# Six matmuls of two k-tiles in another order, in a hybrid decoder step

## The chip, the cores and the metric

The kernel runs on one core of one Trainium2 chip. The metric is the time of one execution in device microseconds, taken over several runs; beside it there is one execution that was recorded by the hardware profiler, with the instructions of every engine.

## The reference

The kernel computes one layer of a hybrid decoder for a prompt of 256 tokens and for 8 samples of 4 tokens, 288 token rows together, with a model width of 2048. Nearly all of its arithmetic is products of the token rows with float32 weights:

```python
xn = _rmsnorm(x, p['norm_mix'])
z, xbc, dt_raw, q, k, v, r, g_lr, gate_a, gate_b = _split(xn @ p['w_in'], IN_SIZES)
...
branch_a = u @ p['w_ssd_out']
...
branch_b = o @ p['w_gla_out']
merged = jax.nn.sigmoid(gate_a) * branch_a + jax.nn.sigmoid(gate_b) * branch_b
h = x + merged @ p['w_mix_out']
h = h + _cross_attend(_rmsnorm(h, p['norm_cross']), mem_k, mem_v, p['w_cq'], p['w_co'])
up = _rmsnorm(h, p['norm_ffn']) @ p['w_up']
...
h = h + (jax.nn.silu(gt) * a) @ p['w_down']
```

Between them stand two recurrences (a state-space scan and gated linear attention), cross-attention into 256 memory tokens, whose keys and values are projections of 256 memory rows, and a causal convolution in the feed-forward part.

## The kernel before, in words

**Three products for one.** TensorE multiplies in the reduced format float32r. To keep float32 accuracy, each operand is split into a high part (the value rounded to float32r) and a low part (the rest, rounded too), and a product becomes three: high by high, high by low, low by high, added up in one PSUM accumulator. The token rows are split once for a stage: `X(k)` gives the pair `xh`, `xl` of k-tile `k`, each 128 x 288. The weights are split as they come: `wload` (L102) brings a block of up to four k-tiles by 256 columns into one of three `raw` buffers by SyncE's queue, and `wsplit` (L94) makes two k-tiles of it into `hi`, a copy on ScalarE (L97), and `lo`, a subtraction on VectorE (L99). There are five buffers for each.

**The loop.** `proj_w` (L114) is a generator for one projection of at most 256 output columns, that is `nt` = 2 accumulators of 128 output columns by 288 token rows, each in a PSUM bank. For each pair of k-tiles it splits the weights and then, for each accumulator, issues six matmuls (L127 to L133). The weights are the stationary operand, 128 x 128, the token rows are streamed, 288 of them. A group of six is called a group in what follows; two groups use one split, and twelve matmuls thus use one `hi` and one `lo`. After the last pair of k-tiles `cons` takes the accumulator out. `yield` after each split lets `weave` (L154) put pieces of the scans or of attention between the groups.

**The order of the work.** Everything on an engine runs in the order of the program; waits between engines are set by a framework, from the tiles that an instruction reads and writes. A `hi` buffer comes free after the last matmul that reads it, and ScalarE then makes the next split into it. Four accumulators rotate, so that one projection can start while the one before is taken out.

**Where it is used.** All projections of token rows run through `proj_w`: `w_in` (rows `xn`), the two output projections of the branches (`un`, 4 k-tiles at a time), `w_mix_out` (`mx`), `w_cq` (`hn`), `w_co` (`co`), `w_up` (`hf`) and `w_down` (`pr`). The projections of the memory rows have a loop of their own, `mem_proj` (L287), in which the rows are the stationary operand and 512 columns of the weights are streamed; the change doesn't touch it. Cross-attention multiplies split operands as well, 256 columns at a time (L1346 to L1348, L1387 to L1389).

In the profile a matmul's operands are named with the streamed one first: `acc<-hf,whi` streams `hf` through the stationary `whi`.

Of the kernel before, what the change touches and what calls it, by code (L numbers as in the profile page):

```python
# [40 lines left out]
def hybrid_step(ctx: ExitStack, tc: tile.TileContext, I: dict, O: list):  # L41
# [3 lines left out]
    MM, TR = nc.tensor.matmul, nc.tensor.transpose  # L45
# [10 lines left out]
    def acc_tile():  # L56
        return ps.tile([P, 512], F32, tag="acc", bufs=4, name="acc")

    def mm_tile():
        return ps.tile([P, 512], F32, tag="mm", bufs=3, name="mm")  # L60
# [33 lines left out]
    def wsplit(raw):  # L94

        hi = wp.tile(list(raw.shape), F32R, tag="whi", bufs=WB, name="whi")
        S.copy(hi, raw)  # L97
        lo = wp.tile(list(raw.shape), F32R, tag="wlo", bufs=WB, name="wlo")
        V.tensor_tensor(lo, raw, hi, ALU.subtract)  # L99
        return hi, lo  # L100
# [8 lines left out]
    def flush():  # L109

        while late:
            late.pop(0)()

    def proj_w(load, ncol, X, nk, cons, N=T):  # L114

        nt = (ncol + P - 1) // P
        accs = [acc_tile() for _ in range(nt)]
        for k0 in range(0, nk, 4):
            kn = min(4, nk - k0)
            raw = load(k0, kn)  # L120
            for s0 in range(0, kn, 2):
                hi, lo = wsplit(raw[:, s0:s0 + 2, :])
                for j in range(nt):
                    m = min(P, ncol - j * P)
                    a = accs[j][0:m, 0:N]
                    cs = slice(j * P, j * P + m)
                    for k in range(2):  # L127
                        xh, xl = X(k0 + s0 + k)
                        MM(a, hi[:, k, cs], xh, start=(k0 + s0 + k == 0), stop=False)  # L129
                        MM(a, hi[:, k, cs], xl, start=False, stop=False)  # L130
                    for k in range(2):
                        xh, xl = X(k0 + s0 + k)
                        MM(a, lo[:, k, cs], xh, start=False, stop=(k0 + s0 + k == nk - 1))  # L133
                    if k0 + s0 + 2 == nk:
                        cons(j, a)
                if k0 + s0 == min(4, nk - 2):
                    flush()
                yield

    def proj(w, c0, ncol, X, nk, cons, row0=0):  # L140
        def load(k0, kn):
            return wload(w[row0 + k0 * P:row0 + (k0 + kn) * P, c0:c0 + ncol].rearrange("(k p) n -> p k n", p=P))
        return proj_w(load, ncol, X, nk, cons)
# [40 lines left out]
    def halves(alloc, name):  # L184

        ts = [alloc(f"{name}{i}") for i in range(2)]

        def at(k, n=None):
            t, o = ts[k // 8], k % 8
            if n is None:  # L190
                return t[:, o, :], t[:, 8 + o, :]
            return t[:, o:o + n, :], t[:, 8 + o:8 + o + n, :]
        return at
# [55 lines left out]
    X = halves(bigr, "xn")  # L249
    with pool("p0") as p0:  # L250
# [207 lines left out]
        def dt_cons(j, a):  # L458
# [4 lines left out]
            V.tensor_tensor(lr3[64:80, :], a[64:80], lr3[64:80, :], ALU.subtract)  # L463

        run(proj_w(dt_load, 112, X, KT, dt_cons))

        def dt_prep():
# [750 lines left out]
    for j2 in range(KT // 2):  # L1218
        def cons(j, a, j2=j2):
            added(hx[j2][:, j, :], 2 * j2 + j, a, vec("norm_cross"), hn, acc)  # L1220
# [198 lines left out]
    a = mm_tile()  # L1419
# [143 lines left out]
    a = acc_tile()  # L1563
# [61 lines left out]
```

## Time and profile before

| what | value |
|---|---|
| runs | 2606.95, 2609.87, 2605.52 us; median 2606.95 |
| profiled execution | 2607.92 us |
| its span, first to last instruction | 2606.2 us |
| mean granted TensorE clock over the span | 0.996 |
| HBM traffic over the span | 196 GB/s |
| matmuls of L129, L130, L133 | 5328 on each line, of 19123 in all |

In the profile, PE is TensorE's matmuls, PEld its weight loads, DVE is VectorE, ACT ScalarE, POOL GpSimd and SP SyncE. Matmuls are pipelined and the end of each is modelled, so a matmul's duration covers part of the next one's: the distance from one start to the next tells the pace. A line of a group reads: line, engine, operation, out<-in, shapes, count, busy time and mean duration in ns, idle time before and what ended it. A line of the timeline reads: start in us, length in us, engine, line, operation, and how many of them were merged.

### The profile page before, as it was taken

Reading aid. Unit: us, or ns where it says so; the run is one execution under the profiler, and the core shown is the slowest. Engines: PE = TensorE matmul, PEld = TensorE weight load, DVE = VectorE, ACT = ScalarE, POOL = GpSimd, SP = SyncE. Lnnn points to the kernel's source line nnn. Section 1 sums busy time; section 2 is a strip of 40 time slices with the busy share of each in tenths; the row PEclk is TensorE's granted clock in tenths of the full one; section 3 lists DMA queues with packets and bytes.
Section 4 is the critical chain, followed back from the end, with each engine's and each line's share of the span. In section 5 each row is a group of like instructions: output and inputs, shape, how many; then the busy total and the mean of one; then the engine's idle time right before and its main releaser. Section 6 shows DMA issues by size and latency. Waiting matters only on the chain. (4 is left out here: it accounts for less than half of the span.)

```text
span 2606.2 us, 50491 instructions
## 1 busy us (share of the span) xinstructions
PE 2576.2 (99%) x19123; PEld 2473.3 (95%) x19123; DVE 1718.2 (66%) x3683; ACT 1376.2 (53%) x2796; POOL 308.2 (12%) x425
## 2 busy tenths in 40 slices
PE   8999999999999999999999999999999999999998
PEld 7889999999989998999999989899999999999998
DVE  5655786886766566666666555567777677675765
ACT  7655655564645463534455544455545454454545
POOL 2003021100000000000000222202202020110200
PEclk9999999999999999999999999999999999999999
DMA  7666566665676666777666778655555555555553
GB/s 250 208 225 205 179 200 179 201 195 148 201 234 212 199 213 218 225 233 237 182 207 214 246 262 298 213 166 168 166 170 166 168 161 172 168 160 178 164 171 126
DMA packets 435280, 514.07 MB, mean 197 GB/s; under 512 B 23208, under 2 KB 384984, under 8 KB 434716
## 3 DMA queue, kind: packets, MB, share of 16 engines
q1 hardware_dynamic: 408684, 423.16, 52.5%
q0 software_dynamic: 26320, 87.68, 10.1%
q8 instruction: 150, 2.46, 0.4%
q14 instruction: 94, 0.77, 0.1%
q10 hardware_dynamic: 32, 0.01, 0.0%
HBM read 465.27 MB, written 45.48 MB: 196 GB/s over the span
## 5 line engine op out<-in xcount | busy, mean ns | idle before, releaser
L99 DVE TENSOR_TENSOR wlo<-raw,whi 128x512 fp32r<-128x512 f32 (+1 forms) x1464 | 989.5, 689 | 703.3 <-ACT whi L97 689.6
L97 ACT CAST whi<-raw 128x512 fp32r<-128x512 f32 (+1 forms) x1464 | 898.2, 618 | 1043.8 <-PE acc L130 824.1
L129 PE MATMUL acc<-xn,whi 128*128 128x288 f32 (+1 forms) x1936 | 551.0, 300 | 2.8 <-ACT whi L97 2.8
L130 PE MATMUL acc<-xn,whi 128*128 128x288 f32 (+1 forms) x1936 | 542.5, 295 | 0.0
L133 PE MATMUL acc<-xn,wlo 128*128 128x288 f32 (+1 forms) x1936 | 413.0, 295 | 1.4 <-DVE wlo L99 1.4
L129 PE MATMUL acc<-hf,whi 128*128 128x288 f32 x1408 | 396.0, 296 | 0.0
L130 PE MATMUL acc<-hf,whi 128*128 128x288 f32 x1408 | 393.5, 295 | 0.0
L129 PEld LDWEIGHTS acc<-xn,whi 128*128 128x128 f32 (+1 forms) x1936 | 365.0, 189 | 10.2 <-issue 6.7
L130 PEld LDWEIGHTS acc<-xn,whi 128*128 128x128 f32 (+1 forms) x1936 | 365.2, 189 | 4.2 <-issue 1.0
L133 PEld LDWEIGHTS acc<-xn,wlo 128*128 128x128 f32 (+1 forms) x1936 | 311.3, 188 | 1.8 <-DVE wlo L99 1.7
L133 PE MATMUL acc<-hf,wlo 128*128 128x288 f32 x1408 | 302.2, 296 | 0.0
L130 PEld LDWEIGHTS acc<-hf,whi 128*128 128x128 f32 x1408 | 265.1, 188 | 0.1
L129 PEld LDWEIGHTS acc<-hf,whi 128*128 128x128 f32 x1408 | 264.7, 188 | 0.1
L133 PEld LDWEIGHTS acc<-hf,wlo 128*128 128x128 f32 x1408 | 225.4, 188 | 0.0
L130 PE MATMUL acc<-pr,whi 128*128 128x288 f32 x704 | 196.6, 295 | 0.0
L129 PE MATMUL acc<-pr,whi 128*128 128x288 f32 x704 | 195.9, 294 | 0.0
L129 PE MATMUL acc<-un,whi 128*128 128x288 f32 x512 | 153.3, 315 | 2.3 <-DVE mb L897 1.0
L133 PE MATMUL acc<-pr,wlo 128*128 128x288 f32 x704 | 147.8, 291 | 0.0
L1457 POOL COPY fsp<-fst 128x16 f32<-128x16 f32 x88 | 105.4, 1222 | 335.3 <-ACT fcg L1463 87.8
L130 PE MATMUL acc<-un,whi 128*128 128x288 f32 x512 | 143.2, 295 | 0.0
L130 PEld LDWEIGHTS acc<-pr,whi 128*128 128x128 f32 x704 | 132.4, 188 | 0.0
L129 PEld LDWEIGHTS acc<-pr,whi 128*128 128x128 f32 x704 | 132.1, 188 | 0.0
(525 smaller groups left out, 4245.3 us busy)
## 6 DMA issues: line engine op xcount, KB each, us to landing
raw<-in_w_in_dram SPq DMA_DIRECT2D x240, 512.0 KB
raw<-in_w_up_dram SPq DMA_DIRECT2D x176, 512.0 KB
raw<-in_w_down_dram SPq DMA_DIRECT2D x88, 512.0 KB
raw<-in_w_ck_dram SPq DMA_DIRECT2D x32, 512.0 KB
raw<-in_w_cv_dram SPq DMA_DIRECT2D x32, 512.0 KB
raw<-in_w_ssd_out_dram SPq DMA_DIRECT2D x32, 512.0 KB
sin<-in_state_gla_dram POOLq DMA_DIRECT2D x32, 512.0 KB, 5.7
out_dram<-sin SPq DMA_DIRECT2D x32, 512.0 KB
```

Source lines behind the costliest of these rows:

```text
L97: S.copy(hi, raw)
L99: V.tensor_tensor(lo, raw, hi, ALU.subtract)
L129: MM(a, hi[:, k, cs], xh, start=(k0 + s0 + k == 0), stop=False)
L130: MM(a, hi[:, k, cs], xl, start=False, stop=False)
L133: MM(a, lo[:, k, cs], xh, start=False, stop=(k0 + s0 + k == nk - 1))
L1457: G.tensor_copy(sp[:, :, 0:2], st.rearrange("p (b k) -> p b k", k=2))
```

## The change

The order of the six matmuls of a group is changed. Before, the two k-tiles' high weights are multiplied by the high and the low rows, one k-tile after the other, and then the two low weights by the high rows. Afterwards the first k-tile goes high weights by low rows, high by high, low by high, and the second the other way around: low weights by high rows, high by high, high by low. `start` and `stop`, which open and close the accumulation, go with the first and the last matmul as before.

```diff
-                    for k in range(2):
-                        xh, xl = X(k0 + s0 + k)
-                        MM(a, hi[:, k, cs], xh, start=(k0 + s0 + k == 0), stop=False)
-                        MM(a, hi[:, k, cs], xl, start=False, stop=False)
-                    for k in range(2):
-                        xh, xl = X(k0 + s0 + k)
-                        MM(a, lo[:, k, cs], xh, start=False, stop=(k0 + s0 + k == nk - 1))
+                    (xh0, xl0), (xh1, xl1) = X(k0 + s0), X(k0 + s0 + 1)
+                    MM(a, hi[:, 0, cs], xl0, start=(k0 + s0 == 0), stop=False)
+                    MM(a, hi[:, 0, cs], xh0, start=False, stop=False)
+                    MM(a, lo[:, 0, cs], xh0, start=False, stop=False)
+                    MM(a, lo[:, 1, cs], xh1, start=False, stop=False)
+                    MM(a, hi[:, 1, cs], xh1, start=False, stop=False)
+                    MM(a, hi[:, 1, cs], xl1, start=False, stop=(k0 + s0 + 2 == nk))
                     if k0 + s0 + 2 == nk:
                         cons(j, a)
```

The new matmuls stand on lines 128 to 133.

## The prediction

> **What bounds the kernel now.** I read the first page from the top: the totals of the engines, the granted clock, the chain of work that ended last.
>
> ```profile
> span 2606.2 us, 50491 instructions
> PE 2576.2 (99%) x19123; PEld 2473.3 (95%) x19123; DVE 1718.2 (66%) x3683; ACT 1376.2 (53%) x2796; POOL 308.2 (12%) x425
> PEclk9999999999999999999999999999999999999999
> PE acc L130 12%; PE acc L133 12%; PE acc L129 12%; DMA frow<-in_ffn_conv_w_dram 0%; PE mm L1548 0%; POOL h L1432 0%; PE la L1380 0%; DVE y L1578 0%; PE mm L1474 0%; PE mm L1447 0%; PE mm L1425 0%; PE acc L1567 0%; PE acc L1566 0%; PE mm L1370 0%; ACT h L1535 0%
> ```
>
> TensorE is busy for 99% of the span, its clock is granted in full in every slice, and the chain consists of the three lines that the change rewrites. So nothing but the pace of these matmuls matters, and a lower power draw could buy no clock. The same row shows that every matmul has its own weight load, 19123 of each, although L130 already uses the weights of the L129 just before it: shared weights are loaded again.
>
> How many matmuls there are, by the tile that they stream (all instructions of L133; L129 and L130 have as many):
>
> ```profile
> L133 PE MATMUL acc<-xn,wlo x1936: 288/295/442, 113.4 to 1346.8; 128*128 128x288 f32 x192, 128*112 128x288 f32 x2
> L133 PE MATMUL acc<-hf,wlo x1408: 288/297/298, 1748.7 to 2488.0; 128*128 128x288 f32 x176
> L133 PE MATMUL acc<-pr,wlo x704: 288/291/298, 1902.3 to 2593.1; 128*128 128x288 f32 x176
> L133 PE MATMUL acc<-un,wlo x512: 288/295/300, 385.2 to 1245.7; 128*128 128x288 f32 x171
> L133 PE MATMUL acc<-mx,wlo x256: 293/296/297, 1347.5 to 1447.9; 128*128 128x288 f32 x128
> L133 PE MATMUL acc<-hn,wlo x256: 288/295/304, 1448.6 to 1619.1; 128*128 128x288 f32 x128
> L133 PE MATMUL acc<-co,wlo x256: 288/295/400, 1621.3 to 1747.9; 128*128 128x288 f32 x128
> ```
>
> They add up to 5328, two in each group of six: **2664 groups of six**. The durations of 290 to 300 ns overlap; what counts is the distance from start to start. The table by stretches of time has a stretch that is almost nothing but these groups:
>
> ```profile
> 1250.00:1470.00 220.00, 220.00 (x1671) 219.89 (x1670) 131.63 (x238) 112.96 (x208) 16.78 (x27) 1.00 0.66 207
> ```
>
> 220 us over 1671 matmuls is 131.7 ns a step, 790 ns a group, so 2664 groups take about 2105 us of the span. An effect of 0.2% of the time (5.2 us, about what a measurement can tell from no change) is 2 ns in a group of 790. That is the scale on which this change is decided.
>
> **The steps of a group.** Before, the order is hi0·xh0, hi0·xl0, hi1·xh1, hi1·xl1, lo0·xh0, lo1·xh1. Steps 1 to 2 and 3 to 4 share weights; the other four, with the one to the next group, share nothing. Afterwards it is hi0·xl0, hi0·xh0, lo0·xh0, lo1·xh1, hi1·xh1, hi1·xl1: still **two** steps that share weights, and **two new ones that share rows** (xh0, xh1). So the change in sharing is only this: two steps of six that shared nothing now stream the same rows twice. Nothing is added or removed: six matmuls, six loads, the same splits, DMAs and evictions.
>
> What sharing weights is worth, from the timeline of TensorE in the first up-projections:
>
> ```profile
> 1777.71 0.29 PE L129 MATMUL acc<-hf,whi 128*128 128x288 f32 x1
> 1777.84 0.29 PE L130 MATMUL acc<-hf,whi 128*128 128x288 f32 x1
> 1777.97 0.29 PE L129 MATMUL acc<-hf,whi 128*128 128x288 f32 x1
> 1778.10 0.29 PE L130 MATMUL acc<-hf,whi 128*128 128x288 f32 x1
> 1778.24 0.43 PE L133 MATMUL acc<-hf,wlo 128*128 128x288 f32 x2
> 1778.50 0.29 PE L129 MATMUL acc<-hf,whi 128*128 128x288 f32 x1
> ```
>
> The steps with shared weights (L129 to L130) are 0.13 long, those without 0.13 to 0.14, and the two of L133 to the next group 0.26 together. At most a few ns lie in it, and the change leaves the number of such steps as it is.
>
> What sharing rows is worth, from the memory projections, which stream 512 rows: L313 and L314 use the same rows with other weights, and so do the two of L317. In a group of six, four steps share rows and two (L314 to L317, and L317 to the next L313) do not.
>
> ```profile
> 150.07 0.39 PE L313 MATMUL acc<-whi,mn_hi 128*128 128x512 f32 x1
> 150.30 0.39 PE L314 MATMUL acc<-whi,mn_lo 128*128 128x512 f32 x1
> 150.52 0.39 PE L313 MATMUL acc<-whi,mn_hi 128*128 128x512 f32 x1
> 150.75 0.39 PE L314 MATMUL acc<-whi,mn_lo 128*128 128x512 f32 x1
> 150.98 0.61 PE L317 MATMUL acc<-wlo,mn_hi 128*128 128x512 f32 x2
> 151.43 0.39 PE L313 MATMUL acc<-whi,mn_hi 128*128 128x512 f32 x1
> ```
>
> The steps that share rows take 0.23, 0.22 and 0.23, the next, which shares none, takes 0.23, and the last two take 0.45 together: all six are alike (1.36 / 6 = 0.227). Sharing rows is worth 0 here. I take **0** for the two new steps. The end on the fast side would be that such a step falls to that of a narrower matmul, 0.120 us at 256 rows (rows below): 11.7 ns x 2 x 2664 = 62 us; the trace speaks against it. Below nothing, the bound is the slow rival's.
>
> The Trainium skill's page "TensorE: Matmul & The Clock Gate", section "Step-by-step: what each phase is for", says that loading is separate from computing so that one load can serve many matmuls, and that loads and streamed rows have two read ports of their own, so that neither takes bandwidth from the other. The first half would favour neighbours with the same weights; the trace has a load for each matmul all the same, so it gives nothing here. The second half speaks against any gain from reading the same rows twice, and the even steps at 512 rows agree. By the same page's section "Back-to-back issue gap", N/2.4 + 2.5 ns, a step of 288 would be 122.5 ns, an estimate; if the two new steps came down to it, the sum would be lower by about 49 us.
>
> **What moves.** Three small things.
>
> The low half is needed at the third matmul of a split and no longer at the fifth, 0.26 us sooner. The high half is released by the last matmul of its twelve and no longer by the tenth, so its refill starts 0.26 us later, and the low half is made from it.
>
> ```profile
> L97 ACT CAST whi<-raw 128x512 fp32r<-128x512 f32 (+1 forms) x1464 | 898.2, 618 | 1043.8 <-PE acc L130 824.1 <-DMA raw<-in_w_in_dram 39.2 <-DMA raw<-in_w_up_dram 30.7
> L99 DVE TENSOR_TENSOR wlo<-raw,whi 128x512 fp32r<-128x512 f32 (+1 forms) x1464 | 989.5, 689 | 703.3 <-ACT whi L97 689.6 <-PE mm L1268 4.1 <-PE mm L1548 2.6
>   DVE wlo L99: 3.1, 2
> ```
>
> ACT stands idle for 824 us until L130 frees a high half: the splits are made as soon as a buffer is free, and there are five. A refill takes 0.62 + 0.69 = 1.3 us; the buffer is due four splits later, 4 x 12 x 0.132 = 6.3 us. About 5 us are spare, of which the change takes 0.26 + 0.26. This cover hides it. It fails only where the split is late for another reason: the third row, from the waits of L133, has 3.1 us in two waits (entries of a load and of its matmul). With a few near misses I bound the loss by 0 and 2 us and take **0.5 us**. Behind a wait of the load nothing but TensorE's own next matmuls is queued.
>
> The first matmul of a projection now wants the low part of the rows, which VectorE makes after the high part: a loss of one step, 0.13 us, at the start of each stage that has just made its rows (eight for `un`, six for `pr`, `mx`, `hn`, `co`, `hf`: some 19), 0 to 2.5 us. The rows of a stage are made well ahead of the first weights in all but a few; I take 0.
>
> The last matmul of an accumulation is at the same place in the group, so evictions, the tail and the stores stay.
>
> **The pace itself.** Where nothing disturbs them, the groups run at one of three paces, and keep it until another kind of instruction comes between. One is the 0.79 above. The others, both in the down-projections:
>
> ```profile
> 2336.91 0.30 PE L129 MATMUL acc<-pr,whi 128*128 128x288 f32 x1
> 2338.52 0.30 PE L129 MATMUL acc<-pr,whi 128*128 128x288 f32 x1
> 2344.25 0.29 PE L129 MATMUL acc<-pr,whi 128*128 128x288 f32 x1
> 2345.03 0.29 PE L129 MATMUL acc<-pr,whi 128*128 128x288 f32 x1
> ```
>
> The first two rows are two groups apart: 1.61, so 0.805 a group. The last two are one group apart: 0.78. Same shapes, same tile, same order, and 3% between them: something that the profile doesn't show picks the pace. A new order may sit differently on it. Its bounds come from these rows: all at 0.78 gives -10 ns x 2664 = -27 us, all at 0.805 gives +15 x 2664 = +40 us. I take **0**: 0.79 is where the stretch without disturbance stays, and the new order has the same kinds of matmuls and loads.
>
> **The sum.** Span 2606.2 + 0.5 = 2606.7; the profiled execution took 2607.92, 1.7 more than its span, which gives 2608.4; it lies 1.0 above the median of the runs, 2606.95. So **2607.4 us**, no change that can be measured.
>
> **The rivals.**
>
> *The pace settles lower.* The groups fall from 0.79 and 0.805 toward the 0.78 that is already seen: 2606.95 - 27 = 2580 if all do, 2593 if half do. For it: the pace exists with these very shapes. Against it: it doesn't last through disturbances. Chance 0.30.
>
> *Row sharing saves time after all*, some 5 ns a step, about half of the 11.7 above: 2 x 5 x 2664 = 27 us, 2580. At 288 rows no row of the trace shows two neighbours with the same rows. Against it stand the even steps at 512. Chance 0.05.
>
> *Slower: the pace goes to the straight line of the other widths.* In cross-attention 256 rows are streamed, with weights shared in one step of three:
>
> ```profile
> 1503.72 0.28 PE L1346 MATMUL mm<-kTh,qh 128*128 128x256 f32 x1
> 1503.84 0.28 PE L1347 MATMUL mm<-kTl,qh 128*128 128x256 f32 x1
> 1503.96 0.28 PE L1348 MATMUL mm<-kTh,ql 128*128 128x256 f32 x1
> 1504.08 0.28 PE L1346 MATMUL mm<-kTh,qh 128*128 128x256 f32 x1
> ```
>
> 0.120 a step there and 0.227 at 512 make 0.417 ns a row, and 120 + 32 x 0.417 = 133.3 ns at 288: 0.800 a group. Today's order runs 10 to 20 ns below this line. If that saving hangs on its sequence, with rows that alternate after each pair, the new one, three steps with tile 0 and three with tile 1, may lose it: +10 x 2664 = +27 us, 2634. It decides from a mean group of 0.792 on. For it: both other widths sit on the line with even steps. Against it: nothing in the trace ties the saving to the order. Chance 0.23.
>
> *The change doesn't do what it says*: every matmul still loads, the rows are still read twice, and sharing is a word in the source only. That is part of my forecast, and gives its time.
>
> **How the numbers follow.** Forecast, within 0.2%: 0.42. Faster: 0.30 + 0.05 = 0.35. Slower: 0.23. The likeliest is 2607.4, with 2602 to 2612 as its own range. For 8 in 10 the range reaches two thirds of the way to the two paces, 18 us each way, where part of the groups has moved: 2588 to 2625.
>
> **What would show it.** The counts of matmuls and loads stay at 19123 each; fewer loads would refute the step on sharing. The waits on the low half stay at a few us; tens of us there would refute the 5 us of cover. The group of six in the stretch from 1250 to 1470 us stays at 0.79; 0.80 or 0.78 there decides for a rival. If the steps with the same rows are shorter than their neighbours by over 2 ns, the zero from the 512 rows was wrong. Idle time of TensorE before the first matmul of a projection would show the low rows as late.

## The result and the profile after

The new order is slower: 2623.66 us in the median against 2608.01 in the same rounds, a ratio of 1.0062 with a 95% interval of 1.0050 to 1.0074. The profiled execution took 2624.54 us, its span 2622.7, which is 16.5 more than before.

From the first page of after, the span, the engines' totals and the chain:

```profile
span 2622.7 us, 49910 instructions
PE 2595.0 (99%) x19123; PEld 2493.0 (95%) x19123; DVE 1714.3 (65%) x3683; ACT 1372.7 (52%) x2796; POOL 253.3 (10%) x425
PEclk9999999999999999999999999999999999999999
PE acc L128 13%; PE acc L131 13%; PE acc L132 13%; PE acc L133 13%; PE acc L130 13%; PE acc L129 13%; PE acc L313 2%; PE acc L314 2%; PE acc L317 2%; PE mm L1268 1%; DMA raw<-in_w_in_dram 1%; PE la L1317 1%; PE la L1380 1%; PE mm L1086 1%; PE mm L1051 1%
```

Matmuls and loads are as many as before, the clock is granted in full, VectorE and ScalarE have the same work. Of the busy times only TensorE's have grown, that of the matmuls by 18.8 us. (The shares of the two chains can't be compared: the one of before covers only 36% of its span, the one of after 93%.)

Where it grew, from the table by stretches of after, once over the output projection and the first queries, once over the middle of the feed-forward part (columns: stretch, its length, busy us and instructions of PE, PEld, DVE, ACT and POOL, granted clock, DMA share, GB/s):

```profile
1250.00:1470.00 220.00, 220.00 (x1651) 219.90 (x1650) 130.37 (x234) 108.64 (x202) 16.80 (x27) 1.00 0.66 205
1950.00:2490.00 540.00, 540.00 (x4056) 539.87 (x4056) 371.39 (x872) 269.98 (x590) 39.66 (x70) 1.00 0.54 166
```

The second stretch in before:

```profile
1950.00:2490.00 540.00, 540.00 (x4088) 539.89 (x4087) 376.74 (x882) 272.51 (x599) 76.17 (x68) 1.00 0.54 167
```

In the first stretch there are 1651 matmuls in 220 us, where there were 1671: 133.25 ns a step and 0.7995 us a group of six, against 131.7 and 0.790 before. In the second, 4056 stand where there were 4088. The same is seen in the timeline of TensorE in the up-projections of after, a group and the start of the next:

```profile
1777.82 0.29 PE L128 MATMUL acc<-hf,whi 128*128 128x288 f32 x1
1777.95 0.29 PE L129 MATMUL acc<-hf,whi 128*128 128x288 f32 x1
1778.08 0.30 PE L130 MATMUL acc<-hf,wlo 128*128 128x288 f32 x1
1778.22 0.29 PE L131 MATMUL acc<-hf,wlo 128*128 128x288 f32 x1
1778.35 0.29 PE L132 MATMUL acc<-hf,whi 128*128 128x288 f32 x1
1778.48 0.29 PE L133 MATMUL acc<-hf,whi 128*128 128x288 f32 x1
1778.62 0.30 PE L128 MATMUL acc<-hf,whi 128*128 128x288 f32 x1
```

The group takes 0.80 us. L128 to L129 and L132 to L133 share weights, L129 to L130 and L131 to L132 share rows, the other two share nothing; all six steps are 0.13 to 0.14.

From the starts of all matmuls in both traces: of the groups that nothing disturbed, before had 465 near 0.78, 1217 near 0.79 and 382 near 0.807, a mean of 0.7912; after, six in seven (1785 of 2079) are at 0.800 and nearly all others just under it, with a mean of 0.7994, and none is near 0.78 and only one near 0.807. The 15,300 undisturbed steps add 19.6 us, the disturbed ones (over 150 ns) give 3.3 back, and everything that isn't a step between two matmuls of `proj_w` takes 492.5 us against 492.3. So the 16.5 us lie in the pace of the undisturbed steps.

### The profile page after: what moved, and what is told of

The parts are those of the page before. It is cut to its first block, busy times and chain, and to the rows that moved or that the text cites. A ratio compares the mean times of both kernels' runs of the same rounds, so it can differ in the third digit from the quotient of the medians.

```text
span 2622.7 us, 49910 instructions
## 1 busy us (share of the span) xinstructions
PE 2595.0 (99%) x19123; PEld 2493.0 (95%) x19123; DVE 1714.3 (65%) x3683; ACT 1372.7 (52%) x2796; POOL 253.3 (10%) x425
## 4 chain that ended last, share of the span: by engine, by line
PE 93%; DMA 2%; DVE 1%; ACT 1%; issue 1%; POOL 0%; SPq 0%; DVEq 0%; ACTq 0%; POOLq 0%
PE acc L128 13%; PE acc L131 13%; PE acc L132 13%; PE acc L133 13%; PE acc L130 13%; PE acc L129 13%; PE acc L313 2%; PE acc L314 2%; PE acc L317 2%; PE mm L1268 1%; DMA raw<-in_w_in_dram 1%; PE la L1317 1%; PE la L1380 1%; PE mm L1086 1%; PE mm L1051 1%
## 5 line engine op out<-in xcount | busy, mean ns | idle before, releaser
L128 PE MATMUL acc<-xn,whi 128*128 128x288 f32 (+1 forms) x968 | 297.2, 307 | 1.5 <-ACT whi L97 1.5
L130 PE MATMUL acc<-xn,wlo 128*128 128x288 f32 (+1 forms) x968 | 286.0, 295 | 2.4 <-DVE wlo L99 2.3
L131 PE MATMUL acc<-xn,wlo 128*128 128x288 f32 (+1 forms) x968 | 286.9, 296 | 0.0
L132 PE MATMUL acc<-xn,whi 128*128 128x288 f32 (+1 forms) x968 | 286.7, 296 | 0.0
L133 PE MATMUL acc<-xn,whi 128*128 128x288 f32 (+1 forms) x968 | 286.4, 296 | 0.0
L129 PE MATMUL acc<-xn,whi 128*128 128x288 f32 (+1 forms) x968 | 286.1, 296 | 0.0
L128 PE MATMUL acc<-hf,whi 128*128 128x288 f32 x704 | 210.6, 299 | 0.0
L132 PE MATMUL acc<-hf,whi 128*128 128x288 f32 x704 | 207.7, 295 | 0.0
L133 PE MATMUL acc<-hf,whi 128*128 128x288 f32 x704 | 207.7, 295 | 0.0
L129 PE MATMUL acc<-hf,whi 128*128 128x288 f32 x704 | 207.7, 295 | 0.0
L131 PE MATMUL acc<-hf,wlo 128*128 128x288 f32 x704 | 207.7, 295 | 0.0
L130 PE MATMUL acc<-hf,wlo 128*128 128x288 f32 x704 | 206.3, 293 | 0.0
L128 PEld LDWEIGHTS acc<-xn,whi 128*128 128x128 f32 (+1 forms) x968 | 182.7, 189 | 8.8 <-issue 6.5
L130 PEld LDWEIGHTS acc<-xn,wlo 128*128 128x128 f32 (+1 forms) x968 | 183.1, 189 | 3.7 <-DVE wlo L99 3.5
L129 PEld LDWEIGHTS acc<-xn,whi 128*128 128x128 f32 (+1 forms) x968 | 182.7, 189 | 3.7 <-issue 1.0
L132 PEld LDWEIGHTS acc<-xn,whi 128*128 128x128 f32 (+1 forms) x968 | 182.5, 189 | 0.1
L133 PEld LDWEIGHTS acc<-xn,whi 128*128 128x128 f32 (+1 forms) x968 | 182.5, 189 | 0.0
L131 PEld LDWEIGHTS acc<-xn,wlo 128*128 128x128 f32 (+1 forms) x968 | 182.3, 188 | 0.2
L130 PEld LDWEIGHTS acc<-hf,wlo 128*128 128x128 f32 x704 | 133.0, 189 | 0.0
L129 PEld LDWEIGHTS acc<-hf,whi 128*128 128x128 f32 x704 | 132.2, 188 | 0.1
```

The lines of the kernel that those rows point to most:

```text
L128: MM(a, hi[:, 0, cs], xl0, start=(k0 + s0 == 0), stop=False)
L129: MM(a, hi[:, 0, cs], xh0, start=False, stop=False)
L130: MM(a, lo[:, 0, cs], xh0, start=False, stop=False)
L131: MM(a, lo[:, 1, cs], xh1, start=False, stop=False)
L132: MM(a, hi[:, 1, cs], xh1, start=False, stop=False)
L133: MM(a, hi[:, 1, cs], xl1, start=False, stop=(k0 + s0 + 2 == nk))
```

## The experiments

The question was what today's order has that the new one lacks. Rows and weights that neighbours share are one thing; another is **which k-tile's rows** are streamed. Before, the tiles follow one another as 0 0 1 1 0 1, after as 0 0 0 1 1 1. A row tile is 288 float32 long, 1152 bytes in each partition, or 4.5 times 256 bytes, so the tiles lie at offsets 0 and 128 within 256 bytes in turn, and the order of the tiles is also an order of offsets. (Offsets are counted from the start of the buffer that holds the row tiles; where that buffer itself lies is not in the profile.)

In all runs the loop of L127 to L133 is replaced by six matmuls, as in the change, unless the text says otherwise. The results side by side; each ratio is to runs of before in the same rounds, whose median is not always that of the first row, and the matmuls are those of the stretch from 1250 to 1470 us:

| run | tiles in order | median, us | ratio to before, 95% interval | matmuls in 220 us | ns a step |
|---|---|---|---|---|---|
| before | 0 0 1 1 0 1 | 2608.01 | | 1671 | 131.7 |
| after | 0 0 0 1 1 1 | 2623.66 | 1.0062 (1.0050 to 1.0074) | 1651 | 133.3 |
| e1 | 0 0 0 1 1 1 | 2624.08 | 1.0071 (1.0056 to 1.0086) | 1650 | 133.3 |
| e2 | 0 0 1 1 0 1 | 2603.37 | 0.9986 (0.9976 to 0.9995) | 1671 | 131.7 |
| e3 | 0 1 0 1 0 1 | 2623.26 | 1.0063 (1.0046 to 1.0080) | 1651 | 133.3 |
| e4, offsets equal | 0 0 1 1 0 1 | 2615.86 | 1.0039 (1.0024 to 1.0054) | 1661 | 132.5 |
| e5, offsets equal | 0 0 0 1 1 1 | 2614.46 | 1.0031 (1.0020 to 1.0043) | 1661 | 132.5 |
| e6, low rows swapped | 0 0 0 1 1 1 | 2603.49 | 0.9989 (0.9980 to 0.9998) | 1672 | 131.6 |
| e7 | 1 1 0 1 0 0 | 2595.67 | 0.9954 (0.9942 to 0.9967) | 1693 | 129.9 |
| e8 | 1 0 1 0 1 0 | 2617.93 | 1.0038 (1.0024 to 1.0052) | 1651 | 133.3 |

### e1, e2, e3: sharing or the order of the tiles

The six matmuls in short, weights first, then rows (so too in e7 and e8):

```diff
 e1
+MM hi0 xh0; MM hi0 xl0; MM lo0 xh0; MM hi1 xh1; MM hi1 xl1; MM lo1 xh1
 e2
+MM hi0 xh0; MM lo0 xh0; MM hi1 xh1; MM lo1 xh1; MM hi0 xl0; MM hi1 xl1
 e3
+MM hi0 xh0; MM hi1 xh1; MM hi0 xl0; MM hi1 xl1; MM lo0 xh0; MM lo1 xh1
```

> All three products of the first k-tile, then all three of the second, as after the change, but no two neighbours share rows (hi0 xh0, hi0 xl0, lo0 xh0, hi1 xh1, hi1 xl1, lo1 xh1); two steps of six share weights, as before and after. Theory 'tiles' (the saving of today's order arises at steps that pass from one k-tile's rows to the other's, four of six before, two of six after): two such steps, so like after, 0.800 us a group, about 2624 us. Theory 'rows' (streaming the same rows twice in a row takes the saving away): no such step, so like before, 0.79 a group, about 2608 us.

> Two steps of six share rows, none shares weights, and the k-tiles change as before (hi0 xh0, lo0 xh0, hi1 xh1, lo1 xh1, hi0 xl0, hi1 xl1: tiles 0 0 1 1 0 1). Theory 'tiles': four passes from tile to tile, so like before, 0.78 to 0.79 a group, about 2608 us. Theory 'rows': like after, 0.800, about 2624 us. Theory 'weights' (the saving hangs on the two steps with the same weights): like after, about 2624 us.

> The k-tiles in turn, nothing shared (hi0 xh0, hi1 xh1, hi0 xl0, hi1 xl1, lo0 xh0, lo1 xh1: tiles 0 1 0 1 0 1). Theory 'tiles': six passes, at or below before's time, 2580 to 2608 us, a group of 0.78 to 0.79. Theory 'rows': no shared rows, about 2608 us. Theory 'weights': no step shares weights, about 2624 us, 0.800 a group.

e1 shares no rows and is as slow as after; e2 shares rows in two steps and weights in none and is a little faster than before. So neither sharing rows costs anything nor does sharing weights save anything, and both theories of sharing fall. Step by step, e2 shows the very sequences of before: the steps 129, 131, 131, 133, 130, 126 ns are among the commonest of either trace, though other weights and other halves of the rows are behind them. From the table by stretches of e2:

```profile
1250.00:1470.00 220.00, 220.00 (x1671) 219.89 (x1670) 131.75 (x239) 111.53 (x208) 16.79 (x27) 1.00 0.67 209
```

e3 was a miss for the theory "tiles" as I had put it: with the most passes from tile to tile it is as slow as after. It runs in another way, three steps of 131 and one of 140 in turn, whose mean is 133.3. Not the number of passes counts, then, but the sequence.

### e4: the same order with the rows elsewhere

```diff
 halves()
             t, o = ts[k // 8], k % 8
+            p = 2 * (o % 4) + o // 4
             if n is None:
-                return t[:, o, :], t[:, 8 + o, :]
-            return t[:, o:o + n, :], t[:, 8 + o:8 + o + n, :]
+                return t[:, p, :], t[:, 8 + p, :]
+            return t[:, p:p + 2 * n - 1:2, :], t[:, 8 + p:8 + p + 2 * n - 1:2, :]
```

`pr` is placed in the same way, `un` is left. The matmuls and their order are those of before.

> The order of before; only the place of the k-tiles' rows in memory is changed, so that both k-tiles of a pair start at the same offset within 256 bytes (a row tile is 1152 bytes a partition, so neighbours start at offsets 0 and 128 in turn; here the even places are filled first). The stage with un is left as it is. Theory 'offsets' (the saving arises where a step passes between rows that start at different offsets): 0.800 a group in every stage but un, about 2622 us. Theory 'tiles' without the offset as its reason, theory 'rows' and theory 'weights': like before, 0.79, about 2608 us.

```profile
1250.00:1470.00 220.00, 220.00 (x1661) 219.90 (x1660) 132.69 (x236) 110.78 (x203) 16.82 (x27) 1.00 0.65 205
```

Moving the rows alone costs 0.4%, in the interval from 0.2 to 0.5: the place of the rows in memory matters, with the same matmuls in the same order. But it is half of what I expected: 132.5 ns a step and not 133.3. Equal offsets were not one case, and the next run shows the two.

### m1: steps by themselves

Ahead of the kernel of before, with only TensorE at work, 48 matmuls for each line; before each line two records of another kind of matmul, so that the first step is longer.

```python
for x, w, a, i in bench(288, [(0, 0), (0, 0), (288, 128), (288, 128), (0, 256), (288, 384)]): MM(a, w, x, start=(i == 0), stop=(i == 47))
```

The pairs are the start columns of the streamed rows and of the weights.

> Ahead of the kernel of before stand 68 sequences of 48 matmuls each on constant data, one source line for each sequence, with nothing but TensorE at work: widths from 128 to 512 rows, and at 288 rows different start places of the streamed rows, in the orders 0 1, 0 0 1 1, 0 0 1 1 0 1 (before) and 0 0 0 1 1 1 (after), with row tiles from 288 to 2592 columns apart. The time is longer by what is added; only the steps count. Theory 'offsets': the same row tile over and over takes N/2.4 + 13.3 ns, 133.3 at 288, whatever its start; 0 0 1 1 0 1 with tiles 288 columns apart takes 130 to 134.5 in the mean, depending on how it begins, and with tiles 1024 columns apart (same offset) 133.3; 0 0 0 1 1 1 takes 133.3 everywhere. Theory 'order alone': 0 0 1 1 0 1 is shorter at any distance. Theory 'other engines' (the saving comes from what VectorE, ScalarE and the DMAs do to the memory meanwhile): every sequence of 288 rows takes 133.3 here, where they are idle.

From the timeline of TensorE of this run (start, length of the whole sequence, line): L68 streams 256 rows, L70 288 from column 0, L72 320; L80 288 rows from column 32, that is 128 bytes, L82 from column 64, 256 bytes. L86 is the order 0 0 1 1 0 1 with tiles 288 columns apart, L87 0 0 0 1 1 1; L114 and L115 are the same two with tiles 1024 columns apart.

```profile
63.88 6.00 PE L68 MATMUL ab<-xb,wb 128*128 128x256 f32 x48
...
76.10 6.56 PE L70 MATMUL ab<-xb,wb 128*128 128x288 f32 x48
...
89.48 7.28 PE L72 MATMUL ab<-xb,wb 128*128 128x320 f32 x48
...
154.03 6.64 PE L80 MATMUL ab<-xb,wb 128*128 128x288 f32 x48
...
167.27 6.56 PE L82 MATMUL ab<-xb,wb 128*128 128x288 f32 x48
...
193.60 6.49 PE L86 MATMUL ab<-xb,wb 128*128 128x288 f32 x48
200.07 6.64 PE L87 MATMUL ab<-xb,wb 128*128 128x288 f32 x48
...
377.35 6.57 PE L114 MATMUL ab<-xb,wb 128*128 128x288 f32 x48
383.89 6.56 PE L115 MATMUL ab<-xb,wb 128*128 128x288 f32 x48
```

Of each length some 0.22 is the first step and 0.29 the last matmul's own duration; the rest are 46 steps. So L86 runs at (6.49 - 0.51) / 46 = 0.130 and L87 at 0.133, with data that never change and with every other engine idle: the theory of other engines falls, and the single steps of L86 (128, 132, 131, 133, 130, 126 ns) are those of before's fast groups. With tiles 1024 columns apart, at the same offset, the two orders are alike, 0.132.

One expectation was wrong: rows that all start at a multiple of 256 bytes run at 131.7 ns (L70, L82), not at 133.3; those that all start 128 bytes beyond run at 133.3 (L80). (The starts at 32, 64 and 192 bytes, from the starts of the matmuls, settle at 133.3, 132.2 and 133.3.) This is the size of e4: there, half of the pairs lie at 0 and half at 128, and (131.7 + 133.3) / 2 = 132.5, as measured.

### e5 and e6: the new order, with the offsets taken away and given back

e5 has the matmuls of after and the places of e4. e6 has the matmuls of after, and only the low rows of the two k-tiles of a pair change places:

```diff
 e6, halves(), and the same for un and pr
-                return t[:, o, :], t[:, 8 + o, :]
+                return t[:, o, :], t[:, 8 + (o ^ 1), :]
```

> The order of after with the places of the rows of e4_same_offsets, where both k-tiles of a pair start at the same offset within 256 bytes: four k-tiles of a half at 0, four at 128 bytes. Theory 'offsets', with the steps that the sequences by themselves gave (131.67 ns where all rows start at multiples of 256 bytes, 133.33 where all start 128 beyond): a mean group of 0.795 in every stage but un, the same as the old order has with these places, so about 2616 us, faster than after by about 8 us. Theory 'tiles' (the order of the tiles counts wherever their rows lie): like after, 0.800, about 2624 us.

> The order of after; only the low rows of the two k-tiles of each pair change places in memory, so that the six streams start at offsets 128 0 0 128 128 0 within 256 bytes, which is the cycle 0 0 1 1 0 1 of before, and no longer 0 0 0 1 1 1. Theory 'offsets': the paces of before come back (0.78, 0.79, 0.805, a mean near 0.79), about 2607 us, 16 us under after, though instructions, sharing and waits are those of after. Theory 'order of the products' (sharing, or where the low weights are needed): like after, 0.800, about 2624 us.

The stretch in e5:

```profile
1250.00:1470.00 220.00, 220.00 (x1661) 219.89 (x1660) 129.27 (x234) 110.56 (x205) 16.79 (x27) 1.00 0.65 208
```

and in e6:

```profile
1250.00:1470.00 220.00, 220.00 (x1672) 219.89 (x1671) 131.30 (x239) 112.20 (x209) 16.78 (x27) 1.00 0.65 208
```

e5 came out at 2614.5 where 2616 was expected, with as many matmuls in the stretch as e4: where both tiles of a pair start at the same offset, the two orders run alike. e6 came out at 2603.5, by the two ratios to before 0.7% under after, with the same sharing and the low weights needed just as early; only the offsets of its six streams are again a turn of 0 0 1 1 0 1. That settles the cause as far as the offsets go: the order of the products acts through the order of the offsets at which their rows begin. (e6 has one subtraction more in each attention head, four VectorE instructions in all, because two swapped tiles don't form one access pattern.)

### m2 and e7: the beginning

The three paces of before were still open. m2 puts 72 matmuls on each line, two tiles 288 columns apart: all cycles of six steps, those with three of each tile with several beginnings, and 24 random orders of twelve steps.

> Ahead of the kernel of before stand sequences of 72 matmuls on constant data, one line each, with two row tiles 288 columns apart, in all orders of two tiles over six steps, the order 0 0 1 1 0 1 begun at each of its six places after four kinds of start, and 24 random orders over twelve steps. Theory 'offsets': 0 0 0 1 1 1 and 0 1 0 1 0 1 and tile 1 alone settle at 133.3, tile 0 alone at 131.67, and 0 0 1 1 0 1 at 130, 131.67 or 134.5 by how it begins, which would be why the kernel shows three paces; if the sequence alone decides, all its starts settle at 130. An order that stays under 130 would be a kernel faster than both.

From its timeline: L70 is 0 0 0 1 1 1; L73 and L81 are 0 0 1 1 0 1 after one and after two matmuls of another kind, L88 is the same cycle begun as 1 1 0 1 0 0.

```profile
73.69 9.84 PE L70 MATMUL ab<-xb,wb 128*128 128x288 f32 x72
...
102.96 9.92 PE L73 MATMUL ab<-xb,wb 128*128 128x288 f32 x72
...
181.38 9.73 PE L81 MATMUL ab<-xb,wb 128*128 128x288 f32 x72
...
250.65 9.62 PE L88 MATMUL ab<-xb,wb 128*128 128x288 f32 x72
```

With the first step and the last duration off, 70 steps are left: one cycle, and three paces, 0.130 (L88), 0.132 (L81) and 0.134 (L73), which are 0.78, 0.79 and 0.807 a group, while 0 0 0 1 1 1 is at 0.133 here and in all its other beginnings on these lines. So before's three paces are the three that its one cycle settles at, and where it begins and what stands ahead of it change which. They aren't all: L86 of m1 is the same order, begun in the same way behind the same kind of matmul as L73, and runs at 0.130 where L73 runs at 0.134; what differs is the weights that the steps load and where the buffers lie. No order that was tried settled under 130.0.

e7 is before's cycle, begun elsewhere:

```diff
+MM hi1 xh1; MM hi1 xl1; MM hi0 xh0; MM lo1 xh1; MM hi0 xl0; MM lo0 xh0
```

> The cycle of before begun at another place: hi1 xh1, hi1 xl1, hi0 xh0, lo1 xh1, hi0 xl0, lo0 xh0 (tiles 1 1 0 1 0 0). Of the sequences by themselves this beginning settled at 130.0 ns in three of five starts and at 131.67 in two, the beginning 0 0 1 1 0 1 at 134.4 in three of six and 131.67 in three. Theory 'offsets and the start decide the pace': more groups at 0.78 and fewer at 0.805 than before, 2585 to 2605 us. If the start inside the kernel is set by other things, the paces are mixed as before, about 2607 us.

```profile
1250.00:1470.00 220.00, 220.00 (x1693) 219.89 (x1692) 132.85 (x240) 112.92 (x209) 16.79 (x27) 1.00 0.65 211
```

2595.67 us, 0.46% under before (interval 0.33 to 0.58%), and the fastest of all: from the starts of the matmuls, some 940 groups run at 0.78 where before had 465, and one near 0.807, where before had 382. It beats both kernels, but not in each stage: with `hf` the mean group falls from 0.797 to 0.784, with `pr` it rises from 0.7825 to 0.7896. A beginning chosen for each stage was not tried.

### e8: a miss

```diff
+MM hi1 xh1; MM hi0 xh0; MM hi1 xl1; MM hi0 xl0; MM lo1 xh1; MM lo0 xh0
```

> The k-tiles in turn as in e3, begun with the second (hi1 xh1, hi0 xh0, hi1 xl1, hi0 xl0, lo1 xh1, lo0 xh0: tiles 1 0 1 0 1 0). By itself the sequence settled at 133.3 ns when it began with tile 0 (three starts) and at 130.0, steps of 128 and 132 in turn, when it began with tile 1 (one start). If the beginning decides inside the kernel too: 0.78 a group in many stages, 2580 to 2600 us. If the cycle settles at 133.3 whatever it begins with: like e3, 0.800, about 2623 us.

2617.9 us lies between the two expectations. The pace of 0.78, with steps of 128 and 132 in turn, does appear in some 230 groups, 173 of them with `hf`; the others run mostly as in e3, at a mean of 0.799. So the beginning matters in the kernel, but one beginning by itself doesn't foretell which pace most stages settle at.

## Why the prediction was right or wrong

**The range and the forecast.** The wide range, 2588 to 2625, holds the 2623.66 by little more than 1 us. It does so because it was drawn two thirds of the way to the slow rival, not because the sum was right: the likeliest time, 2607.4, was 16 us too low, its own range of 2602 to 2612 missed the result, and "no change that can be measured" was wrong.

**The frame held.** TensorE's pace is all that matters, no load is spared, no clock can be won, and 2 ns in a group decide. Of these the counts in the page of after (19123 and 19123) and the granted clock are shown. The chain that I read as "the three lines that the change rewrites" covered only 36% of the span; in after, where it covers 93%, the six lines of the group are 78%.

**Sharing is worth nothing: right, and now shown at 288 rows.** e1 and e2 take sharing of rows and of weights away and put it back, and the time goes with the order of the tiles. As far as sharing goes, this agrees with what the Trainium skill's page "TensorE: Matmul & The Clock Gate" says in the section "Step-by-step: what each phase is for" of read ports of their own. The N/2.4 + 2.5 of the section "Back-to-back issue gap" on this page of the Trainium skill, an estimate of 122.5 ns here, was reached by no sequence of 288 rows; the fastest settled at 130.0. That section of the Trainium skill gives it as the gap of isolated matmuls and says that it counts no loads; the prediction left this out.

**The low weights: not contradicted.** I took 0.5 us, within 0 to 2. The waits of L130, the first to read a low half in after:

```profile
  DVE wlo L99: 5.8, 9
```

That is 5.8 us in nine waits where before had 3.1 in two, which counts a wait of a load and of its matmul each. The matmuls alone, in the waits of before and of after:

```profile
PE acc L133 <- DVE wlo L99: 1.4, 1, 1.4
PE acc L130 <- DVE wlo L99: 2.3, 4, 0.9
```

They waited 0.9 us more. These waits lie in the disturbed steps, which came to 3.3 us less all together, so what they cost at the end isn't separated. The low rows that are now wanted first show in one wait, 0.7 us on the low half of `co`, where before waited 0.4 on its high half; in the waits of after:

```profile
PE acc L128 <- DVE co L170: 0.7, 1, 0.7
```

**The pace: wrong, the step that failed.** "I take **0**: 0.79 is where the stretch without disturbance stays, and the new order has the same kinds of matmuls and loads." The kinds are the same, but the pace hangs on the order of the rows' offsets, and the new one takes the stretch from 0.790 to 0.7995. The term that I put at 0 measured +19.6 us over the undisturbed steps. I had bounded it from the paces that before shows, +40 and -27 us, and the result lies between these. That a pace lasts until something comes between is nearly so: of 1818 pairs of undisturbed neighbouring groups in before, 68 change it.

**The slow rival came true, with its mechanism half named.** It said 0.800 a group, from the straight line through 256 and 512 rows, and that the saving may hang on the order of the tiles. Both hold: 0.7995, and e6 gives the saving back. Its reason, even steps of tiles streamed three at a time, was not the whole: e3, with the tiles in turn, is on 133.3 too, and equal offsets come to 131.7 or 133.3 by where they lie. That the straight line gave just 133.3 was in part luck: in m1 272 and 304 rows settle at 125.4 and 137.8 ns, where the line has 126.7 and 140.0. Its price, 27 us, was too high, because it counted every group from 0.79. The mean of before, 0.7912, has groups at 0.807 that gained, and disturbed steps gave 3.3 us back: 8.2 ns x 2664 = 22 us by the undisturbed mean, 19.6 over the steps that were undisturbed, 16.5 in the span.

**The chance.** I gave it 0.23 and no change 0.42. The line through the other two widths, and two paces within a few us of `pr`, were evidence that the shapes alone don't fix the pace; I weighed "nothing in the trace ties the saving to the order" above it. The two stages with even steps had all their rows at multiples of 256 bytes from the start of their buffers, which the profile doesn't show and the sizes of the tiles do; no run has them elsewhere, so this isn't shown as the reason of their even steps.

**Open.** Why these offsets give these paces, why one cycle has several, and which beginning leads to which, is not settled by any run here.

## What to carry to other kernels

Where TensorE is busy back to back, read its pace as the distance between starts over many steps and compare stages with the same shapes: paces that differ with the same instructions say that something outside the source line sets them. Look at where streamed rows begin in memory before reordering matmuls: 288 float32 make a stride that alternates between two offsets within 256 bytes, and the order of matmuls is then an order of offsets. Neighbours that shared weights or rows gained nothing here, where each matmul has its own load.

## What the runs showed of the hardware that was not expected

- The step of a stream of 288 rows, each with its own load of 128 x 128, depends on the byte offset of its rows: 131.7 ns where all start at multiples of 256 bytes, 133.3 at 128 beyond, and, in m2, with the two offsets mixed, means from 130.0 to 137.8, settled by the end of a sequence.
- Under 256 rows the step soon stops falling: in m1 sequences of 128, 192 and 224 rows all settle at 111.7 ns, 256 at 120.0, 320 at 146.6.
- The first step of 288 rows behind a matmul of plain float32 takes about 215 ns instead of 131 in the sequences of m1 and m2. In the kernel about half of the first steps behind a matmul of another kind (some 180 of 348 in before) are as long.
